# Moving modulation units and S5 table turns between two MLPs in a two-block kernel

## Chip, cores and metric

The kernel runs on one core of one Trainium2 chip. The metric is device time in microseconds of one launch, the median of the runs. All weights come from the chip's memory during the launch; nothing is kept from one launch to the next.

## What is computed

256 tokens of width 1024 go through four residual pairs of mixer and MLP. The first two take shift, scale and gate from a modulation: one product of the condition `c` with a 1024 x 6144 matrix per layer, that is six vectors of 1024 numbers, (layer, 0) to (layer, 5), which every token shares. The mixers are, in order: a convolution with a gated linear recurrence, stick-breaking attention, an S5 state space layer with a gated unit (GLU), and forgetting attention.

```python
def first_block(...):
    c_act = jax.nn.silu(c)
    for layer in range(DEPTH):                       # 2
        mod = c_act @ ada_w[layer] + ada_b[layer]
        shift1, scale1, gate1, shift2, scale2, gate2 = jnp.split(mod[:, None, :], 6, axis=-1)
        h = rms_norm(x, norm_mix[layer]) * (1.0 + scale1) + shift1
        ...                                          # y: the mixer of this layer
        x = x + gate1 * y
        h = rms_norm(x, norm_mlp[layer]) * (1.0 + scale2) + shift2
        x = x + gate2 * (jnp.square(jax.nn.relu(h @ mlp_w1[layer])) @ mlp_w2[layer])

def s5_mixer(u, log_dt, a_re, a_im, b_re, b_im, c_re, c_im, d_skip, w_glu):
    lam_bar = jnp.exp(lam * dt)
    bu = jnp.einsum('blgc,gpc->blgp', uf.astype(jnp.complex64), b_bar)
    _, states = lax.associative_scan(_ssm_binop, (a_elems, bu), axis=1)
    y = jnp.real(jnp.einsum('blgp,gcp->blgc', states, c))
    ...                                              # skip, gelu, GLU
```

## The kernel before

**Stages.** They follow each other by the data: layer 0 (conv and recurrence), m1 (first MLP), sb (stick-breaking attention), m2 (second MLP), S5 with GLU, m3, forgetting attention, m4. In the trace m1 runs from 171.8 to about 358 us, sb to 505, m2 to 701, S5's own part to about 758.

**Weights.** They come as units of 1 MB, 128 x 2048 floats, in the order of `weight_plan`. SyncE (SP) issues a load whenever one of six `raw` buffers is free (`pump`). SP's instructions stay in the order in which they are written, stores among them: an instruction at the head that waits holds all that stand behind it. ScalarE (ACT) rounds a unit to `wh`, VectorE (DVE) takes the rest `wl` = `raw` - `wh`, and TensorE (PE) does three products with the split activations (`hh`, `hl` in an MLP), 48 matmuls of 128 x 256 for a unit.

**MLP.** `mlp()` takes units A(0) to A(15) of the first matrix and B(0) to B(15) of the second: A(u), side work, B(u-1), side work, the last two B together. A(u) is evacuated by DVE (`wb`, `ht`), ACT (two steps on `ht`, then `hh`) and DVE (`hl`). Side work is handed out by generators with a budget for each call.

**Side work.** Three kinds matter here.
- Modulation units ("ada") lie between the MLP's units in the plan. DVE dots each with `crow` in two halves (`ada_dot`), and its `raw` buffer is free again after the second. Twelve units of layer 1's vectors (1,3), (1,4) and (1,2) are in sb's plan, spread by the table `SBA`; m1 has twelve others.
- `s5_pre1` makes S5's powers on DVE.
- `s5_turns` makes, for each of four quarters q, the angles of the chunks by turns: some ten instructions on DVE with 128 x 512 numbers (on `adaacc`, `tmpn`, `sqt`), a change of ACT's function table, three functions on ACT (an absolute value, cosine and sine), and three stores by SP, of M and of two parts of TB, to memory (`dM`, `dTB`). A second table change follows the last.

`s5_pre2`, in m2, makes further tables, which are stored as P, K and Q.

**S5's tables back.** Once m2's side work is through, `mlp()` calls its `after`, here `ready`: it sets `s5_ready`, adds three buffers (`s5X`) and pumps. From there SP loads two P tables, a GLU unit, the T tables (from `dK`, eight loads of 128 KB each, rows of 512 bytes), TB, M, two more P, and, when buffers come free, TB, Q and T again.

**Order.** DVE, ACT and PE get their order from a list scheduler, which sorts by need with offsets (`BACK`); SP and GpSimd keep the written order.

Of the kernel before, what the change touches and what calls it, by code (L numbers as in the profile page):

```python
# [46 lines left out]
def weight_plan():  # L47
# [12 lines left out]

    def mlp(tag, w1, w2, l, extra):
        a, b = [], []
        for u in range(DFF // 256):
            a.append(("w", (tag + "a", u), ("cols", w1, l, [(u * 256, 256)])))
            b.append(("w", (tag + "b", u), ("rows", w2, l, u * 256)))
        if tag in COLS2:
            plan.extend(a + [("w", (tag + "b", u), ("tcol", w2, l, u // 2, u % 2)) for u in range(len(a))])
            return
        n = len(a)
        order = [a[0]]  # L70
        for u in range(1, n - 1):
            order += [a[u], b[u - 1]]
        order[-1:] = [a[n - 1], b[n - 3]]
        order += [b[n - 2], b[n - 1]]
        extra = list(extra)
        out = []
        for i, o in enumerate(order):
            out.append(o)
            if i >= 2 and i % 2 == 0 and extra:
                out.append(extra.pop(0))  # L80
        plan.extend(out + extra)
# [10 lines left out]
    rows("wab", "w_out_ab", 0, 0, D)  # L92
    mlp("m1", "mlp_w1", "mlp_w2", 0, ada(0, 5) + ada(1, 1) + ada(1, 0))
    def unit(name, u, w, index, *c):
        plan.append(("w", (name, u), ("cols", w, index, [(x, 256 // len(c)) for x in c])))

    for u in range(2):
        unit("v", u, "w_qkv", 0, 2 * D + u * 256)
    more = ada(1, 3) + ada(1, 4) + ada(1, 2)
    for i in range(12):  # L100
# [133 lines left out]

SBA = (0, 1, 1, 1, 1, 1, 1, 1, 1, 2, 2, 0)

# [35 lines left out]
class Prog:  # L272
# [1029 lines left out]

    def s5_turns(self):

# [9 lines left out]
        flat = lambda t: t.rearrange("p s j -> p (s j)")  # L1314
        for q in range(4):
            L.copy(M, per(m8, q))
# [408 lines left out]

    def ada_side(self, n):
        for _ in range(2 * n):
            self.ada_next(1)
            yield

# [6 lines left out]
    def st_mlp0(self):  # L1737
        self.mlp("m1", 0, self.mlp_finish(self.mod[0, 5], self.upto(1, self.mod[1, 1])),
                 side=[[(self.ada_side(12), 0)], [(self.s5_pre1(), 2.4), (self.s5_turns(), 2.6)]], before=lambda: self.prep_shift(1, self.mod[1, 0]))

# [6 lines left out]
    def st_mlp1(self):  # L1747
# [6 lines left out]
        def ready():  # L1754
            self.s5_ready = True
            for i in range(3):
# [4 lines left out]
        self.mlp("m2", 1, self.mlp_finish(self.mod[1, 5], (a, self.s5_turn)), after=ready,  # L1761
                 side=[[(self.ada_side(4), 0)], [(self.s5_pre2(), 0)]])

# [56 lines left out]
```

## Time and profile before

| | |
|---|---|
| Median of 3 runs | 1286.39 us (1283.89 to 1287.83) |
| Profiled execution | 1288.14 us, its span 1286.4 us |
| TensorE, busy | 1216.1 us |
| VectorE, busy | 1024.0 us |
| ScalarE, busy | 686.4 us |
| m1 | 171.8 to about 358 us |
| sb | to 505 us |
| m2 | to 701 us |
| S5's own part | to about 758 us |

The span goes from the first to the last instruction of the profiled execution; its own time has 1.7 us more around it. Busy time of an engine excludes the issuing of transfers, so SP shows none. A stage's end is read from the rows of its last matmuls.

### The profile page before, as it was taken

The numbers are of one execution on the slowest core, as the hardware profiler recorded it, in microseconds if no ns is written. First come the engines' busy times: TensorE is split into PE (matmuls) and PEld (weight loads), VectorE is DVE, ScalarE is ACT, GpSimd is POOL, SyncE is SP. The second block draws the span as 40 slices with busy tenths as digits, with TensorE's granted clock in tenths as the row PEclk, the third lists the DMA queues.
The fourth block names the chain that finished last, engine by engine and source line by source line (L and its number), as shares of the span: only waits on it lengthen the run. The fifth ranks groups of instructions, "written<-read, shape, count | busy, mean of one in ns | idle before, by whom it ended". The sixth has DMA issues, their size and how long they took to land.

```text
span 1286.4 us, 22613 instructions
## 1 busy us (share of the span) xinstructions
PE 1216.1 (95%) x9412; PEld 1134.3 (88%) x9412; DVE 1024.0 (80%) x1430; ACT 686.4 (53%) x916; POOL 81.8 (6%) x73
## 2 busy tenths in 40 slices
PE   2999999999989999999999789999999999999997
PEld 2999899999888889999998578888889999888886
DVE  7899999999798978999957847777557885877553
ACT  4545465655656875455555245555445554655442
POOL 0012120000010002000001104000000000100000
PEclk7999999999899999999999999999999999999999
DMA  9867476766756564888879994455544523455510
GB/s 380 339 263 293 188 268 259 267 265 245 270 214 258 196 262 150 325 289 262 273 257 185 163 392 167 164 196 197 196 179 181 197 99 131 164 197 180 213 66 34
DMA packets 63655, 283.85 MB, mean 221 GB/s; under 512 B 8000, under 2 KB 25920, under 8 KB 31936
## 3 DMA queue, kind: packets, MB, share of 16 engines
q1 hardware_dynamic: 63552, 282.40, 61.4%
q8 instruction: 74, 1.21, 0.4%
q14 instruction: 29, 0.24, 0.1%
HBM read 267.70 MB, written 14.68 MB: 220 GB/s over the span
## 4 chain that ended last, share of the span: by engine, by line
PE 75%; DVE 14%; ACT 5%; issue 3%; DMA 2%; POOL 1%; SPq 0%; DVEq 0%; ACTq 0%; POOLq 0%
PE psall L335 74%; DVE wl L312 4%; DVE raw L668 3%; ACT wh L292 2%; DMA raw<-in_wst_dram 2%; PE psall L338 1%; DMA raw<-dK 1%; DVE X L325 1%; DVE xTt L312 1%; DVE tmpn L325 1%; DVE adaacc L312 1%; DVE td L312 1%; POOL tw L786 0%; DVE sbe L325 0%; ACT td L292 0%
## 5 line engine op out<-in xcount | busy, mean ns | idle before, releaser
L335 PE MATMUL psall<-X,wh 128*128 128x256 f32 (+2 forms) x3360 | 726.8, 307 | 32.9 <-ACT wh L292 24.4
L335 PEld LDWEIGHTS psall<-X,wh 128*128 128x128 f32 x3360 | 542.5, 190 | 73.6 <-ACT wh L292 25.0
L335 PE MATMUL psall<-X,wl 128*128 128x256 f32 (+1 forms) x1992 | 556.8, 282 | 2.3 <-DVE wl L312 2.3
L312 DVE TENSOR_TENSOR wl<-raw,wh 128x1024 fp32r<-128x1024 f32 (+1 forms) x264 | 429.8, 1654 | 82.3 <-ACT wh L292 81.8
L292 ACT ACTIVATE wh<-raw 128x1024 fp32r<-128x1024 f32 (+1 forms) x264 | 357.8, 1382 | 199.6 <-PE psall L335 160.8
L335 PEld LDWEIGHTS psall<-X,wl 128*128 128x128 f32 x1992 | 375.8, 189 | 3.9 <-DVE wl L312 3.2
L335 PE MATMUL psall<-hh,wh 128*128 128x256 f32 x512 | 145.7, 288 | 3.2 <-ACT hh L292 3.2
L335 PE MATMUL psall<-hh,wl 128*128 128x256 f32 x512 | 146.0, 286 | 0.0
L335 PE MATMUL psall<-hl,wh 128*128 128x256 f32 x512 | 145.8, 285 | 0.0
L335 PE MATMUL psall<-hid,wh 128*128 128x512 f32 (+1 forms) x432 | 136.2, 372 | 0.0
L546 POOL TENSOR_TENSOR sqat<-sqat,sqt 128x256 f32<-128x256 f32 x52 | 53.4, 1028 | 1034.5 <-ACT sqt L292 1033.2
L335 PE MATMUL psall<-hid,wl 128*128 128x256 f32 x384 | 107.9, 281 | 0.0
L335 PEld LDWEIGHTS psall<-hh,wh 128*128 128x128 f32 x512 | 98.6, 194 | 3.9 <-ACT hh L292 3.4
L335 PEld LDWEIGHTS psall<-hh,wl 128*128 128x128 f32 x512 | 99.1, 194 | 1.2 <-issue 1.2
L335 PEld LDWEIGHTS psall<-hl,wh 128*128 128x128 f32 x512 | 99.1, 194 | 0.2 <-DVE hl L312 0.2
L335 PEld LDWEIGHTS psall<-hid,wh 128*128 128x128 f32 x432 | 78.1, 189 | 15.4
L668 DVE CUSTOM_DVE_ANT_0 raw<-raw,adaacc,prmt 128x1024 f32<-128x1024 f32 x64 | 81.3, 1293 | 0.0
L335 PEld LDWEIGHTS psall<-hid,wl 128*128 128x128 f32 x384 | 72.6, 189 | 0.0
L312 DVE TENSOR_TENSOR tmpn<-tmpn,psall 128x256 f32<-128x256 f32 (+1 forms) x32 | 17.7, 554 | 53.1 <-ACT tmpn L292 53.1
L292 ACT ACTIVATE tmpn<-psall 128x256 f32<-128x256 f32 (+1 forms) x38 | 17.9, 472 | 78.6 <-PE psall L335 78.6
L668 DVE CUSTOM_DVE_ANT_0 raw<-raw,adaacc,adn 128x1024 f32<-128x1024 f32 x32 | 42.2, 1339 | 4.3 <-ACT td L292 4.3
L292 ACT ACTIVATE ht<-ht 128x512 f32<-128x512 f32 x64 | 40.0, 626 | 10.0 <-DVE ht L325 9.2
(344 smaller groups left out, 1234.2 us busy)
## 6 DMA issues: line engine op xcount, KB each, us to landing
raw<-in_wst_dram SPq DMA_DIRECT2D x231, 1024.0 KB, 5.5
dQ<-s5X SPq DMA_DIRECT2D x8, 512.0 KB, 5.1
dP<-s5X SPq DMA_DIRECT2D x16, 256.0 KB, 5.3
s5X<-in_wst_dram SPq DMA_DIRECT2D x4, 1024.0 KB, 13.4
raw<-dK SPq DMA_DIRECT2D x32, 128.0 KB, 9.6
s5X<-in_s5blk_dram SPq DMA_DIRECT2D x8, 256.0 KB, 4.2
s5X<-dP SPq DMA_DIRECT2D x2, 1024.0 KB, 8.0
raw<-dP SPq DMA_DIRECT2D x2, 1024.0 KB, 10.7
```

Source lines behind the costliest of these rows:

```text
L292: i = self.nc.scalar.activation(out=out, in_=in_, func=func, **kw)
L312: return self.nc.vector.tensor_tensor(out=out, in0=a, in1=b, op=op)
L325: return self.nc.vector.scalar_tensor_tensor(out=out, in0=a, scalar=s, in1=b, op0=op0, op1=op1)
L335: return self.in_bank(out, self.nc.tensor.matmul(out, lhsT=l, rhs=r, start=start, stop=stop))
L338: return self.in_bank(out, self.nc.tensor.transpose(out, in_, self.ident))
L546: self.nc.gpsimd.tensor_tensor(out=self.sqa, in0=self.sqa, in1=s, op=ADD)
L668: self.nc.vector.tensor_tensor_reduce(out=w, in0=w, in1=self.crow, scale=1.0 if sc is None else sc, scalar=b, op0=MUL, op1=ADD, accum_out= ...
```

## The change

Six of the twelve modulation units leave sb for m1: all four of (1,3) and two of (1,4). The table `SBA` now has 6 in it, m1's plan takes an extra unit behind two of three of its own instead of behind every second one, and `ada_side` hands out 18 units in a new rhythm. `s5_turns` takes a range: quarters 0 and 1 stay in m1, with smaller budgets, and quarters 2 and 3 come in m2, behind `s5_pre2`.

```diff
@@ weight_plan
-    def mlp(tag, w1, w2, l, extra):
+    def mlp(tag, w1, w2, l, extra, due=lambda i: i % 2 == 0):
...
-            if i >= 2 and i % 2 == 0 and extra:
+            if i >= 2 and due(i) and extra:
                 out.append(extra.pop(0))
...
-    mlp("m1", "mlp_w1", "mlp_w2", 0, ada(0, 5) + ada(1, 1) + ada(1, 0))
+    more = ada(1, 3) + ada(1, 4) + ada(1, 2)
+    early = [more.pop(0) for _ in range(len(more) - sum(SBA))]
+    mlp("m1", "mlp_w1", "mlp_w2", 0, ada(0, 5) + ada(1, 1) + ada(1, 0) + early, lambda i: i % 3 < 2)
...
-SBA = (0, 1, 1, 1, 1, 1, 1, 1, 1, 2, 2, 0)
+SBA = (0, 1, 0, 1, 0, 1, 0, 1, 1, 1, 0, 0)
...
-    def s5_turns(self):
+    def s5_turns(self, first, end):
...
-        for q in range(4):
+        for q in range(first, end):
...
-    def ada_side(self, n):
-        for _ in range(2 * n):
+    def ada_side(self, n, two=0):
+
+        for i in range(2 * n):
             self.ada_next(1)
-            yield
+            yield "more" if two and i % two == 0 else None
...
-                 side=[[(self.ada_side(12), 0)], [(self.s5_pre1(), 2.4), (self.s5_turns(), 2.6)]], before=lambda: self.prep_shift(1, self.mod[1, 0]))
+                 side=[[(self.ada_side(24 - sum(SBA), 4), 9)], [(self.s5_pre1(), 2.0), (self.s5_turns(0, 2), 2.2)]], before=lambda: self.prep_shift(1, self.mod[1, 0]))
...
-                 side=[[(self.ada_side(4), 0)], [(self.s5_pre2(), 0)]])
+                 side=[[(self.ada_side(4), 0)], [(self.s5_pre2(), 0), (self.s5_turns(2, 4), 3.0)]])
```

**DVE at the end of m1.** In these rows `wl_78` is the split of B(13), and the two `TENSOR_REDUCE` begin the evacuations of A(14) (`wb_1492`) and A(15) (`wb_1493`). Before:

```order
L312 TENSOR_TENSOR hl_1488<-ht_1491,hh_1485 128x512
L312 TENSOR_TENSOR wl_78<-raw_69,wh_75 128x2048
L312 TENSOR_TENSOR tmpn<-s5t_141,cstt 128x512
L312 TENSOR_TENSOR sqt<-s5t_140,cstt 128x512
L332 TENSOR_REDUCE wb_1492<-psall 128x2
L312 TENSOR_TENSOR adaacc_135<-sqt,tmpn 128x512
L325 SCALAR_TENSOR_TENSOR ht_1490<-stdbt,wb_1492,psall 128x256
L321 TENSOR_SCALAR adaacc_135<-adaacc_135 128x512
```

After (the rows of `raw_67` are half-unit dots of a moved modulation unit):

```order
L333 TENSOR_REDUCE wb_1492<-psall 128x2
L669 ISA raw_67,mod_4_126<-raw_67,adaacc_136,adn_4_131,prmt 128x1024
L669 ISA mod_4_126 128x1
L326 SCALAR_TENSOR_TENSOR ht_1490<-stdbt,wb_1492,psall 128x256 x2
L333 TENSOR_REDUCE wb_1493<-psall 128x2
L326 SCALAR_TENSOR_TENSOR ht_1491<-stdbt,wb_1493,psall 128x256
L313 TENSOR_TENSOR wl_78<-raw_70,wh_75 128x2048
L313 TENSOR_TENSOR hl_1489<-ht_1490,hh_1486 128x512
L326 SCALAR_TENSOR_TENSOR ht_1491<-stdbt,wb_1493,psall 128x256
```

The split of B(13) stood ahead of A(14)'s evacuation and now stands behind the start of A(15)'s; three more half-unit dots of such units stand ahead of these rows, between the evacuations of A(13) and A(14). Turn 3's steps are gone from here.

**ACT at the end of m2.** The first row is the split of the last A unit, the `ht` and `hh` rows its evacuation, `wh_75` the split of the last B unit. Before:

```order
L292 ACTIVATE wh_74<-raw_71 128x2048 [waits DMAHW6_49,PE_49]
L292 ACTIVATE ht_4855<-ht_4855 128x512 [waits DVE_49]
L292 ACTIVATE ht_4855<-ht_4855 128x512 [waits Activation_49]
L292 ACTIVATE hh_4848<-ht_4855 128x512 [waits Activation_49]
L292 ACTIVATE wh_75<-raw_70 128x2048 [waits DMAHW4_49,PE_49]
```

After (the two `tmpn` rows and `sqt` are the functions of quarter 3):

```order
L293 ACTIVATE wh_74<-raw_68 128x2048 [waits DMAHW0_49,PE_49]
L293 ACTIVATE ht_4819<-ht_4819 128x512 [waits DVE_49]
L293 ACTIVATE tmpn<-sqt 128x512 [waits DMAHW0_49]
L293 ACTIVATE ht_4819<-ht_4819 128x512 [waits Activation_49]
L293 ACTIVATE tmpn<-tmpn,hpi 128x512 [waits Activation_49]
L293 ACTIVATE hh_4812<-ht_4819 128x512 [waits Activation_49]
L293 ACTIVATE sqt<-sqt,cstt 128x512 [waits DMAHW1_49]
L306 ACT_TABLE_LOAD
L293 ACTIVATE wh_75<-raw_67 128x2048 [waits DMAHW6_49,PE_49]
```

Three functions and a table change now stand between the last two splits, and the sine (`sqt`) behind `hh`.

**SP at the end of m2.** `dK` and `dP` are stores by `s5_pre2` where they stand on the left, and loads of S5's tables where they stand on the right. Before:

```order
L1411 DMA dK<-s5Kp 16x2x240 [waits DMAHW2_49]
L1411 DMA dK<-s5Kp 16x2x240 [waits DMAHW3_49]
L376 DMA raw_70<-in_wst_dram 128x2048 [waits DMAHW4_49]
L378 DMA s5X<-dP 128x2048 [waits DMAHW7_49,DMAHW5_49]
L378 DMA s5X<-dP 128x2048 [waits DMAHW6_49,PE_49]
L376 DMA s5X<-in_wst_dram 128x2048 [waits PE_49]
L383 DMA raw_68<-dK 16x16x128 [waits DMAHW0_49,DVE_49]
```

After (`dM`, `dTB`: the stores of quarters 2 and 3):

```order
L377 DMA raw_67<-in_wst_dram 128x2048 [waits DMAHW6_49]
L1338 DMA dM<-adaacc_135 128x512 [waits DMAHW7_49]
L1338 DMA dTB<-tmpn 128x512 [waits DMAHW0_49]
L1338 DMA dTB<-sqt 128x512 [waits DMAHW1_49]
L1338 DMA dM<-adaacc_135 128x512 [waits DMAHW2_49,DVE_49]
L1338 DMA dTB<-tmpn 128x512 [waits DMAHW3_49,Activation_49]
L1338 DMA dTB<-sqt 128x512 [waits DMAHW4_49,Activation_49]
L379 DMA s5X<-dP 128x2048 [waits DMAHW5_49]
L379 DMA s5X<-dP 128x2048 [waits DMAHW6_49,PE_49]
L377 DMA s5X<-in_wst_dram 128x2048 [waits DMAHW7_49,PE_49]
L384 DMA raw_69<-dK 16x16x128 [waits DMAHW0_49]
```

Six stores of the two quarters now stand between the last weight unit of m2 and the first load of S5's tables; the last of them waits for ACT.

## Rows read from the trace of the kernel before

**Rows 1.** The page: each engine's busy us, share of the span, instructions.

```profile
PE 1216.1 (95%) x9412; PEld 1134.3 (88%) x9412; DVE 1024.0 (80%) x1430; ACT 686.4 (53%) x916; POOL 81.8 (6%) x73
```

**Rows 2.** Windows by stage: stretch; length, then busy us per engine, clock, DMA share, GB/s.

```profile
171.00:343.00 172.00, 171.25 (x1425) 171.20 (x1426) 163.02 (x281) 101.98 (x104) 0.78 (x2) 1.00 0.69 257
345.00:355.00 10.00, 8.24 (x47) 8.09 (x47) 5.58 (x9) 3.17 (x7) 0.27 (x1) 0.66 0.98 397
376.00:386.00 10.00, 7.63 (x54) 7.43 (x53) 10.00 (x14) 3.39 (x4) 0.00 (x0) 0.86 0.49 173
412.00:448.00 36.00, 35.88 (x310) 32.19 (x309) 35.61 (x55) 29.72 (x39) 0.00 (x0) 1.00 0.61 234
670.00:701.00 31.00, 31.00 (x261) 31.00 (x261) 20.25 (x29) 14.84 (x19) 2.35 (x3) 1.00 1.13 242
```

**Rows 3.** Lines by form, VectorE, 171 to 345: count | busy us, mean ns of one.

```profile
L312 DVE TENSOR_TENSOR wl<-raw,wh 128x2048 fp32r<-128x2048 f32 x32 | 73.8, 2305 | 7.3 <-ACT wh L292 7.0
L668 DVE CUSTOM_DVE_ANT_0 raw<-raw,adaacc,prmt 128x1024 f32<-128x1024 f32 x15 | 19.0, 1276 | 0.0
L325 DVE SCALAR_TENSOR_TENSOR ht<-stdbt,wb,psall 128x256 f32<-128x256 f32 x32 | 14.2, 477 | 0.0
L668 DVE CUSTOM_DVE_ANT_0 raw<-raw,adaacc,adn 128x1024 f32<-128x1024 f32 x8 | 10.8, 1345 | 0.0
...
L325 DVE SCALAR_TENSOR_TENSOR sqt<-adaacc,sqt 128x512 f32<-128x512 f32 x4 | 2.8, 690 | 0.1
...
L329 DVE COPY adaacc<-s5t 128x512 f32<-128x512 f32 x4 | 1.7, 424 | 0.1
```

**Rows 4.** Timeline, ScalarE, end of m1: start, us, instruction [idle before <-releaser].

```profile
333.82 1.92 ACT L292 ACTIVATE wh<-raw 128x2048 fp32r<-128x2048 f32 x1 [5.02 <-DMA raw<-in_wst_dram]
...
340.93 0.71 ACT L292 ACTIVATE sqt<-sqt,cstt 128x512 f32<-128x512 f32 x1
341.65 1.28 ACT L305 ACT_TABLE_LOAD   x1
342.95 1.91 ACT L292 ACTIVATE wh<-raw 128x2048 fp32r<-128x2048 f32 x1
...
346.07 0.63 ACT L292 ACTIVATE hh<-ht 128x512 fp32r<-128x512 f32 x1
```

**Rows 5.** Timeline, SyncE's queue, end of m1.

```profile
341.66 0.59 SPq L1337 DMA_DIRECT2D dTB<-sqt  x1
342.35 5.19 SPq L376 DMA_DIRECT2D raw<-in_wst_dram  x6
```

**Rows 6.** Waits, TensorE, 340 to 512: waited for, us in total, times, longest.

```profile
PE psall L335 <- DVE sbqk L325: 3.5, 3, 2.4
PE psall L335 <- ACT hh L292: 3.2, 1, 3.2
```

**Rows 7.** Timeline, ScalarE, end of m2.

```profile
685.70 1.28 ACT L292 ACTIVATE ht<-ht 128x512 f32<-128x512 f32 x2
...
689.64 1.91 ACT L292 ACTIVATE wh<-raw 128x2048 fp32r<-128x2048 f32 x1 [1.99 <-PE psall L335]
```

**Rows 8.** Timeline, SyncE's queue, S5's tables.

```profile
661.77 0.85 SPq L378 DMA_DIRECT2D s5X<-dP  x2
...
713.21 0.32 SPq L378 DMA_DIRECT2D s5X<-dTB  x1
```

**Rows 9.** Windows in the loading of S5's tables.

```profile
680.00:684.00 4.00, 4.00 (x36) 4.00 (x35) 2.90 (x2) 1.98 (x5) 0.00 (x0) 1.00 1.23 121
692.00:696.00 4.00, 4.00 (x36) 4.00 (x35) 3.45 (x6) 0.97 (x3) 0.00 (x0) 1.00 1.00 410
701.00:716.00 15.00, 10.10 (x169) 7.66 (x167) 13.23 (x22) 8.88 (x16) 1.67 (x3) 1.00 0.13 37
```

**Rows 10.** Chain of waits in order of time, S5: start, us, what.

```profile
729.21 8.75 DMA raw<-dK
738.03 8.15 DMA raw<-in_wst_dram
```

More of the change, by code (lines that the diff above doesn't have):

```diff
@@ L98, in weight_plan @@
         unit("v", u, "w_qkv", 0, 2 * D + u * 256)
-    more = ada(1, 3) + ada(1, 4) + ada(1, 2)
     for i in range(12):
```

## The prediction

> **What bounds the kernel now.** I read the page's busy times first [rows 1]: TensorE (PE) works 95% of the span, VectorE (DVE) 80%. An average over stages with different limits decides nothing, so next came busy time and clock stage by stage [rows 2]. The first MLP (m1, 171.8 to about 358 us) is bound by PE, 171.25 of 172 us until 343, but DVE is at 163.02 of 172 right behind it. The second mixer (sb, 358 to 505) has PE and DVE level in its steady steps: 35.88 and 35.61 of 36 us in 412 to 448. Late in the second MLP (m2, to 701) PE is full and DVE has 20.25 of 31 us to do. In S5 (701 to 758) neither is full; there the transfers' own rows show who is late. So the change moves DVE work between a stage that has 5% of DVE left, one where PE is level with it, and one where a third of DVE is idle, and what it is worth hangs on waits, not on busy time.
>
> **m1: DVE work.** Six units more are dotted, two half-unit dots each. Eight of these twelve take 1.276 us and four 1.345 us [rows 3]: 8 x 1.276 + 4 x 1.345 = 15.6 us. Two of four turns go away. A turn is six 128x512 two-operand instructions at 0.69 us and four simple ones at 0.42 us [rows 3], 5.8 us, so 11.6 us leave. Net DVE in m1: +4.0, to 167 of 172, 97%. PE stays the bound as long as the new dots are not ahead of something it waits for.
>
> **m1: its end.** Turns 2 and 3 are the ones near the end, and there they cost. At 341.66 and 342.35 [rows 5] the store of turn 3's sine stands at the head of SyncE's queue (SP), and the weight loads behind it only go out after it; ScalarE (ACT) waits 5.02 us for a unit once, and runs the table load between the sine and the next split, so that split starts at 342.95 and the evacuation `hh` at 346.07 [rows 4]. PE waits 3.2 us for it [rows 6]. The clock then falls: in 345 to 355 the granted clock is 0.66 on average [rows 2], between the two levels of 1.2 and 2.4 GHz, after PE had stood still; 10 x 0.34 = 3.4 us more. So 6.6 us are lost at the end of m1. With two turns instead of four the last store comes about two units earlier, and this wait goes. What is late next, by the order of the changed kernel: the split `wl` of unit B(13) stands behind the evacuation of A(15) instead of ahead of that of A(14), with four half-unit dots in front. PE has B(13)'s 32 matmuls without `wl` to cover it (171.25 us for 1425 of them [rows 2], 0.12 each), 3.8 us. Against that stand up to 1.35 us for a dot that is under way when A(15) ends, three half evacuations of 0.48 and the split's 2.31 [rows 3], 5.1 us: about 1.3 us late, 1.5 with the reduction. I take another 1.5 us for weight loads that wait for a modulation unit's dots to free their buffer. So 6.6 - 3.0, about **-3.5 us**; bounds 0 (the new stalls are as long as the old one) and -6.6 (none).
>
> **sb.** The twelve half-unit dots leave here, so DVE loses the same 15.6 us and gets a little back for the first step of turn 2, which the order puts here (0.69 us, [rows 3]). PE however is level with DVE, so little of that reaches the end. What can be had are PE's gaps: it waits 3.5 us for `sbqk` [rows 6], most of it in 376 to 386, where DVE is busy 10.00 of 10 us, PE 7.63, and the clock falls to 0.86 [rows 2], 1.4 us more. That is 4.9; I take **-5.0**; bounds -3 (the wait goes, not quite all of it) and -8 (gaps of other names give 3 us more).
>
> **m2.** Turn 2 sits at its start, turn 3 late, where a third of DVE is idle; that DVE work is hidden. ACT is not: at the end of m2 ACT now has, between A(15)'s evacuation from 685.70 and the last split `wh`, that began at 689.64 [rows 7], three more functions of about 0.7 us and a table load of 1.28 us [rows 4]. Behind 1.28 us for the two steps of `ht` and 0.63 for `hh` that makes 685.70 + 1.28 + 0.63 + 2.1 + 1.28 = 691.0: the split starts about 1.3 us later. PE was full until 701 [rows 2], so it may take part of that: +0.5, bounds 0 and 1.5. In the rows of m1's end the split at 342.95 starts 0.02 us after the load's 1.28 us are over [rows 4]. The Trainium skill, "ScalarE: Activation LUTs", section "What ACT_TABLE_LOAD costs", counts 1.28 us for the load and about 1.38 us for a drain, 2.66 us for each switch; by it this term would be 1.4 us larger, and the rows disagree with it.
>
> **S5: its loads.** This is the term that decides. SP issues in a fixed order. Before, the loads of S5's tables start at 661.77 (two P tables, then the glu unit, two T, TB, M and two P) [rows 8], far under m2. Now turn 3's stores stand ahead of them, as the order shows, and the last one waits for turn 3's sine on ACT, which stands behind A(15)'s relu and `hh`: 685.70 + 1.28 + 0.63 + 3 x 0.7 is about 689.7 [rows 4, 7]. So the first load goes out at about 690 instead of 661.77, **28 us later**. Does that matter? The queue runs full from 662 to 701: the T tables, in eight loads each of short rows, move 121 GB/s at a share of 1.23, whole units 410 GB/s at 1.00 [rows 9]. Then it stands nearly idle, a mean share of 0.13 in 701 to 716 [rows 9], since the second batch (TB, Q, T) starts only at 713.21 [rows 8], when S5 has freed buffers. That idle time, 15 x 0.87 = 13 us, is the cover. The second batch starts when the first is through: 690 + 39 = 729 instead of 713.2, and what follows is bound by transfers: the chain runs over the T load of 729.21, 8.75 us, and a unit, 8.15 us [rows 10]. So S5 ends 28 - 13 = 15 us later if nothing else gives, less a microsecond or two for ramps: **+13.5 us**. Lower bound +5: PE and DVE, not the queue, pace S5, and the T load of 8.75 us drops out of the chain, 13.5 - 8.75. Upper bound +17: the ramps cost nothing and the cover is 2 us shorter, because buffers come free late too.
>
> The T tables go in rows of 512 bytes. The Trainium skill, "DMA: Bandwidth & Descriptors", section "Specifications", gives 512 bytes as enough for line rate. The row above (121 against 410 GB/s) disagrees. By the page each T table would take about 2.6 us (its 410 GB/s), the two batches would have 24 us more of cover, and the S5 term would be near nothing and the sum near 1278; as the row is of the very loads, I go by the row.
>
> **The sum.** -3.5 - 5.0 + 0.5 + 13.5 = **+5.5** on the profiled run (1288.14 us, a span of 1286.4 and 1.7 around it), which lies 1.75 above the median of 1286.39. Against the median: 1291.9. A measurement can tell about 0.3% (3.9 us) from no change: under 1282.5 is faster, over 1290.3 slower.
>
> **Rivals.**
> - *The loads' delay is mostly hidden.* S5 in 701 to 746 is also a chain of PE, DVE and ACT, and the first P tables are wanted only after m2. For it: the queue had 13 us idle there, and parts of the delayed batch (M, the last P) are wanted late. Against it: the chain of waits itself names the T load and the unit behind it [rows 10]. Then S5 costs +5 and the sum is -3.5 - 5 + 0.5 + 5 = -3: 1283.4, at the edge of faster; with the larger gains in m1 and sb (-6.6 and -8) -9, 1277. Faster.
> - *Gains and loss cancel.* sb and m1 give near their upper bounds (-6 and -8) and S5 its +13.5: the sum with m2's 0.5 is 0, 1286.4. It decides when the stalls left in m1 are under 1 us.
> - *m1 gives nothing or loses.* DVE at 97% in m1; each modulation unit holds one of six buffers until DVE dots it, 18 times instead of 12, and ACT waits for the next unit behind it. For it: DVE is at 95% before, and one wait of 5 us for a load cost the whole end of m1 [rows 4]. Against it: the dots go out in DVE's gaps up to then and PE had none of these waits until 343. At +3 instead of -3.5, with sb -4, m2 +0.5 and S5 +14: +13.5, 1299.9. It decides from the point where m1's DVE work passes PE's, 4 us more than worked out above.
> - *The change does not move what it says.* If turn 3's sine were done before A(15), the loads would go out earlier by an evacuation and more, and S5 cost +5 to +10. The order of ACT shows it behind A(15), so little is left for that; it goes with the first rival.
>
> **How the numbers follow.** The S5 delay at full size with middling gains, 0.42, 1289 to 1294; the m1 rival 0.16, 1294 to 1300; cancelling 0.22, 1283 to 1289; the hidden delay 0.20, 1277 to 1283. The likeliest gives **1291.9**. The bounds of the terms give 1280 to 1300; with a tenth left out on either side, the range is 1281 to 1299. Slower holds most of the forecast and all of the m1 rival: 0.52. Same: 0.28. Faster: 0.20.
>
> **What the profile after would show.** P's loads issued near 690 minus what m1 and sb gave, just after a store of TB; the queue idle for no 12 us after m2's end; the chain in S5 with more of T and TB waits, and S5 about 13 us longer. PE's `hh` wait at m1's end gone, the clock there at 1.0, sb's DVE busy 15 us less and the `sbqk` wait shorter. The prediction is wrong in its step on S5 if the P loads go out at 690 and S5 is longer by under 5 us, and in its step on m1 if waits for raw units show on ACT through m1.

## The result, and the profile after

The changed kernel takes **1297.16 us** (median of 5 runs, 1294.41 to 1299.91); the kernel before took 1287.19 beside it (1283.89 to 1289.05). The ratio is 1.0079, with a 95% interval of 1.0065 to 1.0094: about 10 us slower. The prediction said slower, 1291.9, with a range of 1281 to 1299.

The profiled execution after has a span of 1295.4 us, before 1286.4: 9.0 us to explain. The page of after gives each engine's busy us, its share of the span and its instructions, and further down the chain that ended last by engine, as shares of the span:

```profile
PE 1221.4 (94%) x9412; PEld 1137.4 (88%) x9412; DVE 1023.5 (79%) x1430; ACT 689.1 (53%) x917; POOL 82.2 (6%) x73
...
PE 68%; DVE 14%; DMA 7%; ACT 6%; issue 3%; POOL 1%; SPq 0%; DVEq 0%; ACTq 0%; POOLq 0%
```

Against [rows 1] every count is the same but ACT's, which has one more instruction. PE executes the same 9412 matmuls and is busy 5.3 us longer; its mean granted clock over the span is 0.979 instead of 0.983, which is about that much (1216.1 x 0.983 / 0.979 is 5.0 more). The other 3.7 us of the 9.0 are gaps.

To say where, I cut both timelines at seven marks that the program itself sets (the split of m1's first unit on ACT; the second evacuation of m1 on DVE; the first `xTt`, the residual, of m1's finish; the third `sbwb` reduction, where the first q and k are evacuated; the last `sbwb`; the first `xTt` of m2's finish; the split of the weight unit that follows S5's tables). The marks lie where they can be found in every kernel, so the stretch called m2 also holds the last steps of sb, from about 468 to 505. Lengths between marks in us, worked out from the starts in the timelines:

| stretch | before | before, once more | after | after, once more | difference of the first two |
|---|---|---|---|---|---|
| ahead of m1 | 151.4 | 153.4 | 151.2 | 151.2 | -0.2 |
| m1, its start | 28.07 | 28.06 | 30.02 | 30.04 | **+1.95** |
| m1, the rest | 173.2 | 172.9 | 171.5 | 171.9 | **-1.7** |
| sb, its start | 27.3 | 27.3 | 32.2 | 32.1 | **+4.9** |
| sb, the rest | 88.4 | 86.8 | 86.5 | 86.1 | **-1.9** |
| m2 | 226.3 | 226.3 | 227.0 | 226.9 | **+0.7** |
| S5 | 70.0 | 68.2 | 75.3 | 72.1 | **+5.3** |
| behind it | 521.8 | 521.8 | 521.8 | 521.7 | 0 |

The second columns are a second profile of the same two kernels (the runs before_again and after_again below). Both starts, m1 and m2 repeat within 0.4 us here; sb's rest within 1.6, S5 within 3.2, and the part ahead of m1 within 2. So S5's loss is 2 to 7 us (72.1 or 75.3 against 70.0 or 68.2), that of sb's rest is not clear, and the starts' losses are the sharpest in the table.

**The starts of m1 and sb.** The prediction has no term for these 6.9 us. (It foresaw 0.69 us of turn 2 in sb, which stands at 384.3, behind what follows here.) Windows of before at both starts (stretch; length, then busy us of PE, weight loads, DVE, ACT and POOL, granted clock, DMA share, GB/s):

```profile
170.00:175.00 5.00, 3.25 (x25) 3.20 (x26) 5.00 (x6) 3.04 (x5) 1.78 (x2) 1.00 0.54 188
...
364.00:370.00 6.00, 6.00 (x50) 5.84 (x49) 6.00 (x5) 4.11 (x7) 0.17 (x1) 1.00 0.43 150
```

and of after, with the windows that answer to [rows 2] at m1's end, sb's first steps and sb's steady steps:

```profile
170.00:175.00 5.00, 4.01 (x19) 3.90 (x20) 4.63 (x5) 2.65 (x4) 0.95 (x3) 0.66 0.52 200
345.00:355.00 10.00, 10.00 (x86) 10.00 (x85) 8.60 (x12) 5.52 (x7) 0.25 (x1) 1.00 1.01 419
364.00:370.00 6.00, 3.79 (x15) 3.62 (x16) 5.90 (x6) 2.22 (x2) 2.00 (x3) 0.66 0.50 178
370.00:376.00 6.00, 6.00 (x43) 6.00 (x41) 3.10 (x4) 3.30 (x6) 0.00 (x0) 0.77 0.52 175
...
376.00:386.00 10.00, 8.85 (x75) 8.65 (x74) 8.72 (x15) 5.08 (x6) 0.00 (x0) 1.00 0.49 163
412.00:448.00 36.00, 34.91 (x292) 31.50 (x291) 32.61 (x48) 30.54 (x40) 0.00 (x0) 1.00 0.44 158
```

In 364 to 370 PE executes 15 matmuls where before it executed 50: it stands still for 2.2 us of the six, and the rest run at a mean granted clock of 0.66, and still 0.77 in the six us behind. At m1's start it is the same on a smaller scale: 19 matmuls instead of 25, although PE is busy longer, since the clock is 0.66 instead of 1.00. What it stood for is in the waits of PE in 340 to 520 of after (waited for, us in total, times, longest), beside [rows 6]:

```profile
PE psall L336 <- POOL sqat L547: 3.2, 1, 3.2
PE psall L336 <- DVE sbqk L326: 3.0, 3, 1.1
PE psall L339 <- DVE sbvt L326: 1.8, 1, 1.8
```

`sqat` is POOL's sum of squares for the norm. It waits for ACT's squares `sqt`, which come with the split activations `X`. ACT's timeline after, at sb's start (start, us, instruction, then idle time before it and what ended that):

```profile
359.61 1.90 ACT L293 ACTIVATE wh<-raw 128x2048 fp32r<-128x2048 f32 x1
...
361.81 0.40 ACT L293 ACTIVATE sqt<-xTt 128x256 f32<-128x256 f32 x1
...
364.45 0.42 ACT L293 ACTIVATE sqt<-xTt 128x256 f32<-128x256 f32 x1 [1.13 <-POOL sqat L547]
```

and DVE's, where the split of sb's first unit stands ahead of the last three `X`:

```profile
361.55 2.29 DVE L313 TENSOR_TENSOR wl<-raw,wh 128x2048 fp32r<-128x2048 f32 x1
363.76 2.68 DVE L326 SCALAR_TENSOR_TENSOR X<-xTt,mod,X 128x256 fp32r<-128x256 f32 x3
```

Before, ACT's timeline had the split earlier by one pair of `X` and `sqt`, and its last square waited for nothing:

```profile
357.61 1.90 ACT L292 ACTIVATE wh<-raw 128x2048 fp32r<-128x2048 f32 x1
...
362.70 0.40 ACT L292 ACTIVATE sqt<-xTt 128x256 f32<-128x256 f32 x1
```

and DVE's `wl`, at 363.50, had one `X` behind it, not three. So POOL had its squares spread out and PE its matmuls; now both come in a lump behind the splits. POOL's own timeline, before and after, has the three sums that decide:

```profile
360.36 2.48 POOL L546 TENSOR_TENSOR sqat<-sqat,sqt 128x256 f32<-128x256 f32 x3 [1.62 <-ACT sqt L292]
...
362.36 3.79 POOL L547 TENSOR_TENSOR sqat<-sqat,sqt 128x256 f32<-128x256 f32 x3 [1.65 <-ACT sqt L293]
```

After, the first of the three begins inside DVE's `wl` (361.55 to 363.84) and takes 2.06 us, the others 0.79 each (their starts, 362.36, 364.50 and 365.36, say the same); before, none of the three begins inside a split. It is so in all 13 traces: at the starts of m1 and sb the 23 sums that begin inside a `wl` take 2.05 to 2.65 us, the 159 others 0.73 to 1.25. So some 1.3 of PE's 3.2 us go with that meeting of POOL and DVE. No run changes it alone, so that DVE's split is what holds the sum is likely, and not shown.

No instruction was added ahead of this pause; the list scheduler sorts by need, and units and turns in other places can give these another rank (the runs below bear on that). PE's pause is then paid a second time by the clock, which stands at 0.50, the lower of its two levels, through 368 to 372. The second half of that:

```profile
370.00:372.00 2.00, 2.00 (x12) 2.00 (x11) 0.16 (x1) 0.89 (x1) 0.00 (x0) 0.50 0.54 98
```

(columns as above). Before, PE stood 1.3 us in 361 to 364; after, 3.2 us in 361 to 368. So of the 4.9 us about 1.9 are waiting and about 3 the clock. At m1's start PE waits once for `sqat`, 2.0 us against 1.9 before, so there most of the 1.95 us is the clock.

**S5.** SP's queue after, beside [rows 8]: turn 3's last store, then the tables; below the gap the first load of the second batch.

```profile
692.12 0.32 SPq L1338 DMA_DIRECT2D dTB<-sqt  x1
692.49 0.92 SPq L379 DMA_DIRECT2D s5X<-dP  x2
...
694.00 19.69 SPq L384 DMA_DIRECT2D raw<-dK  x16
...
718.67 0.32 SPq L379 DMA_DIRECT2D s5X<-dTB  x1
```

The chain of waits there (start, us, what), where before it held two transfers [rows 10], is transfers for 61.6 us on end:

```profile
693.50 11.66 DMA s5X<-in_wst_dram
705.18 8.19 DMA raw<-dK
713.38 7.54 DMA raw<-dK
...
720.99 20.84 DMA raw<-dK
...
741.89 5.93 DMA raw<-dK
...
747.88 7.20 DMA raw<-in_wst_dram
```

and DVE, in its timeline, stands still for one of them:

```profile
723.28 1.29 DVE L313 TENSOR_TENSOR adaacc<-psall,raw 128x512 f32<-128x512 f32 x2 [6.31 <-DMA raw<-dTB]
```

So S5's transfers end last nearly all the way, as predicted, but S5 is longer by 5.3 us (2 to 7 with the second profiles) and not by 13.5.

### The profile page after: what moved, and what is told of

Same layout as the page of the kernel before. It is cut to its first block, busy times and chain, and to the rows that moved or that the text cites. A ratio compares the mean times of both kernels' runs of the same rounds, so it can differ in the third digit from the quotient of the medians.

```text
span 1295.4 us, 22619 instructions
## 1 busy us (share of the span) xinstructions
PE 1221.4 (94%) x9412; PEld 1137.4 (88%) x9412; DVE 1023.5 (79%) x1430; ACT 689.1 (53%) x917; POOL 82.2 (6%) x73
## 4 chain that ended last, share of the span: by engine, by line
PE 68%; DVE 14%; DMA 7%; ACT 6%; issue 3%; POOL 1%; SPq 0%; DVEq 0%; ACTq 0%; POOLq 0%
PE psall L336 67%; DVE wl L313 5%; DMA raw<-dK 3%; DVE raw L669 3%; DMA raw<-in_wst_dram 3%; ACT wh L293 3%; PE psall L339 1%; DMA s5X<-in_wst_dram 1%; DVE X L326 1%; DVE td L313 1%; POOL sqat L547 1%; ACT adaacc L293 0%; DVE tmpn L326 0%; POOL tw L787 0%; DVE xTt L313 0%
## 5 line engine op out<-in xcount | busy, mean ns | idle before, releaser
L293 ACT ACTIVATE tmpn<-psall 128x256 f32<-128x256 f32 (+1 forms) x38 | 17.9, 472 | 78.6 <-PE psall L336 78.6
```

The costliest lines, as they stand in the source:

```text
L293: i = self.nc.scalar.activation(out=out, in_=in_, func=func, **kw)
```

## The experiments

Ratios are to the kernel before on the same chip, with 95% intervals. The lengths by stage come from the one profile of each:

| kernel | ratio | m1 start | m1 | sb start | sb rest | m2 | S5 |
|---|---|---|---|---|---|---|---|
| before | 1 | 28.1 | 173.2 | 27.3 | 88.4 | 226.3 | 70.0 |
| after | 1.0079 [1.0065, 1.0094] | 30.0 | 171.5 | 32.2 | 86.5 | 227.0 | 75.3 |
| units_only | 1.0121 [1.0105, 1.0136] | 30.1 | 189.7 | 25.3 | 85.7 | 226.3 | 68.7 |
| turns_only | 1.0047 [1.0030, 1.0065] | 28.1 | 166.1 | 31.6 | 89.6 | 227.0 | 74.1 |
| both_par | 1.0113 [1.0097, 1.0129] | 30.1 | 171.8 | 32.0 | 86.2 | 237.4 | 66.5 |
| turns_par | 1.0080 [1.0065, 1.0095] | 28.1 | 166.1 | 31.8 | 88.3 | 237.2 | 67.9 |
| both_hold | 1.0038 [1.0020, 1.0055] | 30.0 | 175.5 | 32.0 | 86.4 | 227.0 | 67.1 |
| turns_hold | 0.9988 [0.9974, 1.0003] | 28.1 | 166.1 | 31.6 | 88.3 | 227.9 | 67.4 |
| units_early | 1.0040 [1.0024, 1.0056] | 28.1 | 172.1 | 28.5 | 84.7 | 227.0 | 75.9 |
| early_hold | 0.9998 [0.9987, 1.0010] | 28.1 | 171.8 | 30.1 | 85.9 | 228.5 | 67.1 |
| three_hold | 0.9996 [0.9982, 1.0011] | 28.1 | 171.3 | 28.6 | 85.5 | 227.1 | 67.3 |

### Each part alone

units_only moves the units and leaves all four turns in m1:

```diff
-... (self.s5_turns(0, 2), 2.2)]] ...
+... (self.s5_turns(0, 4), 2.2)]] ...
-                 side=[[(self.ada_side(4), 0)], [(self.s5_pre2(), 0), (self.s5_turns(2, 4), 3.0)]])
+                 side=[[(self.ada_side(4), 0)], [(self.s5_pre2(), 0)]])
```

> The change without its second half: the six units go to the first MLP (m1), but all four turns stay there too. The theory that S5's loss comes from the stores of turn 3 ahead of its loads expects S5's first table loads at about 662 us plus what m1 and sb lose, as in the kernel before, and no longer S5. The theory that the moved units cost what was lost at the borders expects PE's wait of about 2 us at the start of m1 (clock near 0.66 in 170 to 175) and the 3 us wait for the sum of squares at the start of sb again. m1 has 163 + 16 us of DVE work in 172 us, so m1 itself should be 7 to 12 us longer than before; in all 5 to 13 us slower than before. The rival, that the border losses come from the turns, expects neither wait.

It takes 1300.26 us, ratio 1.0121. m1 is 16.5 us longer than before: with six units more and nothing gone, the turns are not through when the matmuls are. The chain of waits at m1's end says how it is paid (start, us, what):

```profile
362.15 7.66 DMA dTB<-tmpn
369.84 0.88 DVE tmpn L326 x2
```

m1's finish writes to `tmpn`, which turn 3's store still reads. PE waits 12.1 us in one piece for the `X` that follow. S5 is 68.7, as before, so S5's loss belongs to the turns; the start of m1 is 30.1, so that loss belongs to the units. sb's start is 2.0 shorter than before, its rest 2.6; this may be what the units give, but sb starts here behind a stall of 12.1 us, so it is not shown.

Two things missed what was expected. The kernel is 14.6 us slower than the one before beside it (1285.69), not 5 to 13. And PE's wait of 3 us for the sum of squares at sb's start did not come: it is 0.9. So the moved units alone do not bring the loss there.

turns_only is the other half, the kernel before with two turns moved:

```diff
-... (self.s5_pre1(), 2.4), (self.s5_turns(), 2.6)]] ...
+... (self.s5_pre1(), 2.4), (self.s5_turns(0, 2), 2.6)]] ...
-... [(self.s5_pre2(), 0)]])
+... [(self.s5_pre2(), 0), (self.s5_turns(2, 4), 3.0)]])
```

> The change without its first half: the units stay in sb, two of four turns go to m2, behind the other S5 work. Theory: the wait for hh at the end of m1 goes (6.6 us with the clock), the start of sb stays as before, and S5 loses 5 us again since its loads start near 690 us: -1 us against before, between -3 and +1. The rival that S5 loses the whole shift of the loads (13.5 us, as was predicted) expects +7.

It takes 1291.72, ratio 1.0047. m1 is 7.1 us shorter: the wait for `hh` and the low clock behind it [rows 2, 6] cost 6.6 by the prediction, and they are gone. But 4.3 of it is lost again at once, at sb's start. Windows there:

```profile
345.00:355.00 10.00, 10.00 (x86) 10.00 (x85) 10.00 (x21) 5.51 (x11) 3.21 (x4) 1.00 0.29 106
356.00:362.00 6.00, 3.48 (x21) 2.88 (x20) 6.00 (x8) 3.33 (x5) 4.34 (x3) 0.84 0.17 30
362.00:368.00 6.00, 6.00 (x33) 6.00 (x34) 3.77 (x5) 3.30 (x6) 0.00 (x0) 0.59 0.70 273
```

PE waits 1.9 us for `sqat` and then runs 33 matmuls in six us. So sb's start is hurt by the turns alone as well, by whatever sets another order there. That was not expected ("the start of sb stays as before"), and with it the time missed: 6.0 us slower than the kernel before beside it (1285.69), where -3 to +1 was expected. The rival of +7 is near for a reason that did not hold: S5 is 4.1 longer and not 13.5. The two parts do not add: -7.1 in m1 here, +16.5 there, and -1.7 for both together. Only together do they leave m1 near its old length.

### S5's tables: earlier, by two ways

The prediction's deciding step was that turn 3's stores hold the loads. both_par gives the turns a budget of their own beside `s5_pre2`, so that they are through long before:

```diff
-... [(self.s5_pre2(), 0), (self.s5_turns(2, 4), 3.0)]])
+... [(self.s5_turns(2, 4), 3.0)], [(self.s5_pre2(), 0)]])
```

> The whole change, but turns 2 and 3 run in m2 beside the other S5 work from its start, not behind it, so that their stores are issued long before S5's table loads. Theory: S5 is as long as before (its loads start near 665 us), m2's end has no functions ahead of the last split: 5 to 6 us less than the changed kernel, 1291 to 1292, still 3 to 5 us over before. Rival: S5 is longer in the changed kernel for another reason (the units, or buffers in another order): then about 1297 again. If DVE, nearly full in early m2, becomes late there, m2 loses 1 to 5 us.

It takes 1299.98 us, ratio 1.0113, where 1291 to 1292 was expected. S5's loss is gone (66.5), and m2 is 10.4 us longer than after; 1 to 5 had been allowed for. Windows in m2 of the kernel before (the first two) and of both_par:

```profile
560.00:600.00 40.00, 40.00 (x359) 37.85 (x357) 38.48 (x40) 20.92 (x26) 0.00 (x0) 1.00 0.85 281
600.00:640.00 40.00, 40.00 (x359) 37.87 (x358) 38.72 (x39) 21.15 (x27) 0.00 (x0) 1.00 0.83 272
...
560.00:600.00 40.00, 37.41 (x308) 35.05 (x306) 33.44 (x38) 18.97 (x22) 0.00 (x0) 0.96 0.73 248
600.00:640.00 40.00, 37.22 (x314) 34.43 (x315) 36.79 (x36) 18.77 (x27) 0.00 (x0) 0.96 0.78 262
```

The kernel before has 40.00 of PE and 359 matmuls in each of these stretches, and DVE at 38.5 and 38.7 of 40: little room for the turns. In both_par PE's waits between 510 and 700 are small ones, 5.7 us in all, for `hl`, `s5X`, `wl`, `ht` and `hh`, and the clock falls to 0.96 in both stretches. So the order of after, turns behind `s5_pre2`, is the better one for m2, and its price is S5.

turns_par does the same to turns_only:

> Only the two turns move, into m2 beside the other S5 work from its start. Theory: the wait for hh at m1's end goes, sb and S5 stay as before: 4 to 7 us faster than before, about 1281. Rival: the end of m1 and the start of sb are bound by the chain over the norm of sb, so that what m1's end gains is lost there: within 2 us of before. If DVE becomes late in early m2, 1 to 5 us are given back.

It came out at 1295.57, ratio 1.0080, and missed what was expected, 4 to 7 us faster, of which early m2 might take 1 to 5 back. m2 is 237.2 again. The middle of m2 is full in both kernels, with the units moved and without.

both_hold keeps after's order of the work and moves the loads alone. SP issues the first five tables (two P, the GLU unit, two T) between the stores of quarter 2 and those of quarter 3; the pump stops at TB, which needs quarter 3:

```diff
-        while self.issued < (end or len(self.plan)):
+        while self.issued < (end or len(self.plan)) and self.issued != self.stop_at:
...
+        def early():
+            self.stop_at = self.pos["TB", 0]
...
-... (self.s5_turns(2, 4), 3.0)]])
+... (self.s5_turns(2, 3, False), 3.0), (early(), 0), (self.s5_turns(3, 4), 3.0)]])
```

(The `False` leaves out a change of ACT's function table that the next quarter would take back; `early` further does what `ready` did.)

> The changed kernel, but S5's first five table loads (two P, the glu unit, two T) are let out between the stores of quarter 2 and those of quarter 3, so that only TB, M and the last P stay behind the store of turn 3's sine. Theory that S5's loss comes from the loads standing behind that store: first P load near 668 us instead of 692, S5 4 to 5 us shorter, in all about 4.5 us under the changed kernel. Rival: S5 loses because its chain of TB, M and the second batch is late, not the first five loads: 0 to 1 us gained. A third possibility: the store of turn 3's sine, now queued behind the T loads, lands late and holds up the reuse of its buffers at the end of m2: 2 to 5 us lost there.

1290.72 (12 runs), ratio 1.0038: half of the loss is taken back. S5 is 67.1, 8.2 shorter than after (5.0 shorter than in after's second profile), and SP's queue shows it:

```profile
671.64 0.90 SPq L1339 DMA_DIRECT2D dTB<-sqt  x1
672.58 1.23 SPq L379 DMA_DIRECT2D s5X<-dP  x2
673.91 0.65 SPq L377 DMA_DIRECT2D s5X<-in_wst_dram  x1
674.65 21.57 SPq L384 DMA_DIRECT2D raw<-dK  x16
696.84 0.34 SPq L1339 DMA_DIRECT2D dM<-adaacc  x1
```

The same loads, 20 us earlier (26 against m2's start), ahead of the stores that held them, with m2 as long as after's. ACT loads its function table 13 times in both traces, at the same places in the work. So the place of the loads in SP's queue is what differs, with the buffers handed over for it, and the intervals of the two ratios do not meet: this shows the prediction's mechanism most plainly. Its profiled execution (1294.92) is 4 us above its median; m1 is 4 us longer in it than in after, though the order of m1's instructions is the same. The granted clock was 0.85 in 300 to 310, 1.00 in after; what set that off in this execution is open. turns_hold puts the same into turns_only:

> Only the two turns move (the units stay in sb), with the same five loads let out ahead of quarter 3's stores. Theory: m1's end is 4.5 us earlier as with the turns moved alone, the start and the end of sb take about 3 of that back, m2's end takes 1, and S5 takes nothing: 0 to 1 us faster than the kernel before, 4 to 5 under the turns moved alone. Rival (S5's loss is not due to the first five loads): no better than the turns moved alone, 4 to 6 us over before.

1284.18 (12 runs), ratio 0.9988 with an interval that holds 1: S5 67.4, and what is left is m1's -7.1 against sb's start of +4.3 and m2's +1.6.

### The starts

The order of after at m1's start has m1's first own modulation unit one place later in the plan (`i % 3 < 2` skips i = 2, which `i % 2 == 0` took). units_early puts it back; as the units are handed out in turn, each of the 18 then comes one place earlier, down to the last, which stands behind A(14) instead of A(15):

```diff
-... + early, lambda i: i % 3 < 2)
+... + early, lambda i: i == 2 or i % 3 < 2)
```

> The changed kernel with one modulation unit more at the front: the first extra unit of m1 stands behind its third own unit, as in the kernel before, and the rest as changed. The order then has a half-unit dot ahead of the last activations at the start of m1 again, and there the order is that of the kernel before. Theory that the lump of three activations behind the split costs the 1.7 us at m1's start: the clock in 170 to 175 is 1.00 again and m1 starts 1.7 us earlier, and at the start of sb, where two activations stand behind the split instead of three, the wait for the sum of squares is shorter than 3.2 us. In all 2 to 5 us under the changed kernel. Rival: the later clock drops and waits are due to how late the units' dots are: no gain, within 1.5 us of the changed kernel.

1290.25, ratio 1.0040. m1's start is 28.1 again, 1.9 shorter than after, and sb's start 28.5, 3.7 shorter. Windows at both:

```profile
170.00:175.00 5.00, 3.16 (x24) 2.90 (x24) 5.00 (x5) 3.05 (x5) 3.51 (x3) 1.00 0.17 34
362.00:370.00 8.00, 5.93 (x44) 5.25 (x43) 8.00 (x12) 3.73 (x8) 3.62 (x3) 1.00 0.29 95
```

PE still stands for 1.84 us in the first and 2.1 in the second, there in pieces of at most 0.8, and the clock stays at 1.00. PE's wait for `sqat` at sb's start is 0.8 us instead of 3.2. DVE's timeline shows why: a half-unit dot is ahead, and two `X`, not three, are left behind the split:

```profile
361.08 1.34 DVE L669 CUSTOM_DVE_ANT_0 raw<-raw,adaacc,adn 128x1024 f32<-128x1024 f32 x1
...
364.29 2.28 DVE L313 TENSOR_TENSOR wl<-raw,wh 128x2048 fp32r<-128x2048 f32 x1
366.49 1.82 DVE L326 SCALAR_TENSOR_TENSOR X<-xTt,mod,X 128x256 fp32r<-128x256 f32 x2
```

One place more at the front of the plan thus decides over 5.6 us at two stages' starts 190 us apart. All 18 units move with it, those at the end of m1 too, so it is not shown that the first unit is what changes sb's start. That the order there is another is shown; why the scheduler sorts it differently was not followed further, and in turns_only, with the units as in the kernel before, that start is slow as well.

### Both repairs, and how many units

early_hold is units_early with both_hold's loads; three_hold is that with three units moved instead of six (`SBA` with nine in it).

> Both repairs on the changed kernel: the unit more at the front of m1, and S5's first five table loads let out ahead of quarter 3's stores. Theory that the two losses are separate and add: each was about 5 us under the changed kernel, so about 10 under it, 0 to 2 us faster than the kernel before by the medians, 3 to 5 by the stages of the profiles (sb -3.5, m2's end +0.8, S5 -2). Rival, that both repairs shorten the same wait: no better than one of them, 4 to 5 us over before.

> As with both repairs, but three units move to m1 instead of six (the table of sb holds nine). Theory that a unit's dots cost in m1 about what they give in sb, since VectorE is nearly full in both: m1 3 to 4 us shorter, sb 3 to 4 longer, the same total within 2 us. Rival, that m1's late dots are the larger cost: 2 to 4 us faster than with six.

1285.59, ratio 0.9998, and 1284.26, ratio 0.9996, 12 runs each. The repairs add up (1.0079 - 0.0041 - 0.0039 is 0.9999), and the loss is accounted for. What the change should bring is not there, however: six units, three, and none (turns_hold) lie within each other's intervals. The stages say where: moving units makes m1 171 to 172 instead of turns_hold's 166.1, and sb's start and rest together 113 to 116 instead of its 120. What is lost at one place is about what is won at the other. But that a unit's dots are what costs and gives is not shown: against six units (early_hold), three should have made m1 3 to 4 us shorter and sb as much longer, and they made m1 0.5 and sb 1.9 shorter. None of the kernels is faster than the one before by more than the intervals.

### The same two kernels again

> The kernel before, profiled a second time, to see how far the stage times of one profile can be read. If they are repeatable, m1's start, m1, the start of sb, the rest of sb, m2 and S5 each come within 0.5 us of the first profile (28.1, 173.2, 27.3, 88.4, 226.3 and 70.0 us). If the stages vary by 2 us or more, differences of that size between the kernels say nothing.

> The changed kernel, profiled a second time: if repeatable, 30.0, 171.5, 32.2, 86.5, 227.0 and 75.3 us within 0.5 us each, with PE's wait of 3.2 us for the sum of squares at the start of sb and the falls of the clock behind it in the same places.

One profile more of each, for the table of the result: 1286.47 and 1293.92 us. Not all stages came within the 0.5 us expected, and so they set the bounds for reading single profiles here: a difference of 2 us in sb's rest or ahead of m1, or of 3 in S5, is nothing. The starts and m2 kept within 0.2 us and m1 within 0.4, but not everywhere: m1 is 4 us longer in both_hold than in after, and sb's start is 28.5 in units_early and 30.1 in early_hold, with the same order of instructions in each pair.

## Why the prediction was half right

| term | predicted | measured |
|---|---|---|
| m1 | -3.5 | +0.2 (start +1.95, rest -1.7) |
| sb | -5.0 | +3.0 (start +4.9, rest -1.9) |
| m2 | +0.5 | +0.7 |
| S5 | +13.5 | +5.3 (2 to 7 with the second profiles) |
| sum | +5.5 | +9.0, with the -0.2 ahead of m1 |

The sign was right, and the range held the time. But two errors of opposite sign, 11.7 us too much of gains and 8.2 too much of loss, hide in that: that the time lies within the range is in good part luck. The range itself was added up short: the terms' bounds give 1277 to 1302 (-9.6 and +15.5 on 1286.4), not 1280 to 1300.

**m1's end, right; its size, short.** The `hh` wait and the low clock behind it were worth 6.6 by the prediction; turns_only shows 7.1, and 345 to 355 after has PE at 10.00 and the clock at 1.00, where it had 8.24 and 0.66 [rows 2]. The stalls that the units bring were put at 3.0; between turns_only and after, m1's rest is 5.4 longer. PE waits twice for a `wl`, 1.6 us at 304.7 and 1.1 at the end, and 0.8 for a `wh`. The prediction costed one late split, B(13)'s; there are two. The sign that it gave against this step, ACT waiting for raw units in m1, tells nothing: before, ACT waited for them 7 times, 19.2 us in all, of which [rows 4] shows one, and after 6 times, 17.9.

**The starts, missed.** The step that failed is "PE stays the bound as long as the new dots are not ahead of something it waits for", taken for granted at the two entries, where no edit is written. There the new places of the units (at m1's start, by units_only) and of the turns (at sb's start, by turns_only) changed the order of instructions that are not theirs. It is 4.9 of sb's error of 8.0 us and 1.95 of m1's 3.7. The changed order could have been read there as it was at the ends; the clock behind the pauses, the larger part of the loss, could not.

**sb's rest.** The gap of 376 to 386 has shrunk as predicted: PE is at 8.85 instead of 7.63 and the clock at 1.00 instead of 0.86 [rows 2]. (381 to 391, which lies nearer the same work, has 8.85 and 1.00 too.) DVE's work did leave sb: 119.2 us in 358 to 508 instead of 131.8 in 358 to 505. But the wait for `sbqk`, which the prediction took to go, stays: the longest is 1.1 us instead of 2.4, yet the three together are 3.0 instead of 3.5 [rows 6], and that for `sbvt` is 1.8 instead of 1.4. In 412 to 448 DVE has 3.0 us less to do, and PE executes 292 matmuls instead of 310 (303 in 414 to 450). "What can be had are PE's gaps" took DVE for the cause of all of them. Of the -5 there are -1.9, in a stretch that varies by 1.6 from profile to profile.

**m2, right.** Near its end ACT's functions of quarter 3 and their table load stand between the evacuation and the last split, these two last:

```profile
692.11 1.28 ACT L306 ACT_TABLE_LOAD   x1
693.41 1.91 ACT L293 ACTIVATE wh<-raw 128x2048 fp32r<-128x2048 f32 x1
```

The split begins 3.77 us later than before [rows 7], of which 3.05 were there already at m2's start (the table's first five stretches): +0.72. Again it starts 0.02 us after the table load of 1.28; the prediction took that row and not the 2.66 us of the Trainium skill, "ScalarE: Activation LUTs", section "What ACT_TABLE_LOAD costs", and the row above agrees with the 1.28 and not with the page.

**S5: the mechanism right, the size not.** The first load goes out 30.7 us later by the clock of the trace, 27.7 against m2's start, where 28 were predicted, right behind turn 3's store. The step that failed is "the second batch starts when the first is through". It was put at 729; it came at 718.67, which is 715.6 without the 3.05, only 2.4 later than before [rows 8]. The second batch waits for buffers that S5's own first steps free, and those need only the first tables, not all of them. So the queue held both batches at once and never ran idle between them: 62.6 us from the first load to the last unit's landing at 755.08, where the prediction had 39 and 33 in a row. Some 4 of these 9.4 us are the rate of the second batch's T tables. Windows after, with the first batch's T tables in the queue (the first row) and the second batch's (the other):

```profile
705.00:710.00 5.00, 2.65 (x12) 1.47 (x12) 4.44 (x10) 3.19 (x8) 1.67 (x3) 1.00 1.22 124
...
740.00:745.00 5.00, 4.29 (x60) 2.45 (x53) 3.86 (x6) 1.92 (x4) 1.97 (x2) 0.86 1.18 165
```

16 loads of 128 KB are 2.1 MB, 17 us at 124 GB/s, about the rate of [rows 9], and 13 at 165. The other 5 us I did not take apart; a unit of m2 ahead of the first batch before, and the second start of the queue at 713 [rows 8], are candidates. Both rows of T loads stay far under the 410 GB/s of whole units [rows 9], against the Trainium skill, "DMA: Bandwidth & Descriptors", section "Specifications". (410 GB/s is this trace's rate, not a figure of the page.) The lower bound of the term, +5, is what came, though not for the reason that stood beside it: S5 is still paced by its transfers.

**The rivals.** "The loads' delay is mostly hidden" had S5 right and the sign wrong, for it kept the gains. "m1 gives nothing or loses" had the time nearest (1299.9) and m1 nearly right; its reason, DVE work past PE's in m1, is true of units_only (DVE 189.9 and PE 184.3 of 201 us in 171 to 372) and not of after (DVE 171.1 and PE 178.0 of 181.7 in 171 to 352.7). Neither had the starts.

## What to carry to other kernels

Where a scheduler orders by need, read the new order at the first steps of every stage that the change's table touches, not only where an instruction was added; at a stage's entry, with its chain over several engines, PE's pause was paid twice here, in waiting and in clock. A store that waited at the head of SP's queue delayed all loads behind it, by 27.7 us; moving the loads past the store was worth 0.4% here (both_hold against after) and 0.6% beside the turns alone. Where two batches of transfers move together, work out what the queue needs for all of it, not the sum of two stretches with an idle one between.

## What was unexpected of the hardware

**A pause of PE and the clock behind it.** PE's first instruction behind the pause at m1's start, before and after:

```profile
171.75 0.70 PE L335 MATMUL psall<-sqat,onesd 128*128 128x256 f32 x2 [1.86 <-POOL sqat L546]
...
170.99 0.91 PE L336 MATMUL psall<-sqat,onesd 128*128 128x256 f32 x2 [2.02 <-POOL sqat L547]
```

At m1's start PE waited 1.86 us before and 1.84 in units_early, and the granted clock in 170 to 175 was 1.00; after it waited 2.02, and the clock was 0.66. At sb's start 3.2 us were followed by 0.66 and 0.77. But in turns_only a single wait of 1.9 us, with short gaps around it, was followed by 0.59, and in [rows 2] 2.4 us by 0.86. So the length of one wait does not tell what follows. Nor do the instructions: early_hold has units_early's order on all four engines at sb's start and the same three waits of PE (0.6, 0.6 and 0.8 us), but where units_early's clock stayed at 1.00 in 362 to 370, early_hold's fell:

```profile
362.00:370.00 8.00, 6.53 (x38) 5.94 (x37) 7.18 (x6) 2.52 (x5) 2.88 (x2) 0.79 0.45 152
```

Its start of sb is 1.6 us longer. So of the 3.7 us that units_early wins there, 1.6 did not come in a second kernel with the same work. What decides is open.

What the clock took in these cases is of the size of the wait itself (an estimate, busy time times what the clock lacks to 1.00, from the windows): 4.01 x 0.34 = 1.4 us at m1's start; 3.79 x 0.34 + 6 x 0.23 = 2.7 at sb's start; 3.48 x 0.16 + 6 x 0.41 = 3.0 in turns_only.

**The same loads at different rates.** T loads, in rows of 512 bytes and alone in the queue, moved 121 GB/s before [rows 9] and 124 in after's first batch, but 165 in its second, and 163 to 166 in both_hold's first (688 to 696). Packets are as small in both. The second batch before was again at the lower rate, 115 in 728 to 732 and 122 in 732 to 736. No run here separates what makes the difference.
